# adaLN sums moved from VectorE to GpSimd, and 512-column products on [high | low] in the mixers and feed-forwards

## The chip, the cores and the metric

The kernel runs on one core of a Trainium2 chip. The metric is the device time of one execution in microseconds. The kernel before took 1213.28 us in the median of 3 runs (1211.68 to 1213.52).

## The reference, cut to what matters

Two layers, each a half-step SwiGLU feed-forward, a gated mixer of three attentions, and a second half-step feed-forward. Each of these six sub-layers is modulated by a vector `c` (adaLN), and the kernel numbers them as stages 0 to 5: 0, 2, 3 and 5 are feed-forwards, 1 and 4 mixers.

```python
D_MODEL = 1024; SEQ = 256; DEPTH = 2; D_FF = 2816        # batch 1, all float32

def swiglu(h, wg, wu, wd):
    return (jax.nn.silu(h @ wg) * (h @ wu)) @ wd
...
for l in range(DEPTH):
    mod = (jax.nn.silu(c) @ w_ada[l] + b_ada[l]).reshape(Bn, 3, 3, D_MODEL)[:, :, :, None, :]
    def pre(xx, j):
        return rmsnorm(xx, norm_gain[l, j]) * (1 + mod[:, j, 1]) + mod[:, j, 0]
    h = pre(x, 0)
    x = x + 0.5 * mod[:, 0, 2] * swiglu(h, w_ffn_gate[l, 0], w_ffn_up[l, 0], w_ffn_down[l, 0])
    h = pre(x, 1)
    (q_sb, k_sb, v_sb, q_dil, k_dil, v_dil, q_swa, k_swa, v_swa,
     g_sb, g_dil, g_swa) = jnp.split(h @ w_in[l], split_idx, axis=-1)
    ...
    merged = (jax.nn.sigmoid(g_sb) * (o_sb @ w_br_sb[l])
              + jax.nn.sigmoid(g_dil) * (o_dil @ w_br_dil[l])
              + jax.nn.sigmoid(g_swa) * (o_swa @ w_br_swa[l]))
    x = x + mod[:, 1, 2] * (merged @ w_out[l])
    h = pre(x, 2)
    x = x + 0.5 * mod[:, 2, 2] * swiglu(h, w_ffn_gate[l, 1], w_ffn_up[l, 1], w_ffn_down[l, 1])
return rmsnorm(x, final_gain)
```

## The kernel before, in words

Every large product is made of three: weights and activations are each split into a high half (rounded to fp32r) and a low half (the rest), and high x high, low x high and high x low are added in PSUM. Activations lie with features on the partitions and the 256 tokens as columns: `hH` and `hL`, 8 blocks of 128 features each.

The work comes in units. A column unit is 128 output features over all 1024 inputs, a row unit is 128 inputs over 1024 outputs. SyncE loads raw weights, two units at a time, into 3 buffers (`load_raws`, L133). `feed` makes the halves five units ahead (`AHEAD`): ScalarE casts `wH` (L150), VectorE subtracts `wL` (L158), 1024 columns each. `step` runs one unit: feed, one tick of the adaLN pace, the matmuls, then what was left over from the unit before, then this unit's own post-work.

A column unit (`aform`, L594) is 24 matmuls of 256 columns: for each of 8 blocks `wH` with `hH` and `wL` with `hH`, then 8 times `wH` with `hL`. In a feed-forward a gate and an up unit share a PSUM bank; the post-work after the up unit is a Silu from PSUM (L652), the product with the up half (L653), a cast to `ffH` (L656) and the low half `ffL` (L657). In a mixer two query, key or gate units share a bank. Row units (`run_rows`, L706) have 12 matmuls of 512 columns, with activations as the stationary side. The last four of them, `TAIL`, run output piece by output piece, so that the residual and the next norm can begin. In the norm, `rstd` (L464 to L467) uses GpSimd.

adaLN is 18 chunks of 1024 columns. The first two are made in a special opening; the other 16 come as 128 steps. A step (`ada_step`) loads 128 x 1024 of `w_ada` into one of two buffers (L260, SyncE), scales it by a column of silu(c) and adds it to an accumulator: ScalarE for the first of a chunk (L281), VectorE for the other seven (L283). A finished chunk is reduced over partitions on TensorE (`ada_reduce`): chunks listed in `filler` in a stage's tail, the others `SOON` ticks after the last step. `PACE` gives the weights by which a stage's steps are spread over its units; `N1` says how many tail reductions stand ahead of the second half's norm.

A `tile` name in the rows leaves buffer numbers out: `pf`, `pq`, `pg` are PSUM banks of feed-forward, query/key and gate units, `pd` those of row units, `acc` an adaLN accumulator, `ada` its load.

## Time and profile before

| | |
|---|---|
| median of 3 runs | 1213.28 us |
| the profiled execution | 1215.12 us |
| its span, first to last instruction | 1213.4 us |
| TensorE matmuls, weight loads busy | 1181.0 us (97%), 1102.9 us (91%) |
| VectorE, ScalarE, GpSimd busy | 837.3 us (69%), 616.0 us (51%), 19.0 us (2%) |
| DMA | 287.55 MB, 237 GB/s in the mean |

The page gives each engine's busy time, the granted clock and the DMA load over the span; the views of the trace give single groups, waits and stretches. The granted clock is a share of 2.4 GHz: 1.00 is that level, 0.50 the other, 1.2 GHz. Matmuls overlap, so that the mean duration of one is longer than the distance to the next; the distance is read from a long piece of the chain, time over count.

### The profile page before, as it was taken

How to read it: one execution, taken by the hardware profiler on the slowest of the kernel's cores; microseconds unless marked ns; L12 is line 12 of the kernel's file. 1: busy time of each engine (PE TensorE's matmuls, PEld its weight loads, DVE VectorE, ACT ScalarE, POOL GpSimd, SP SyncE). 2: the span in 40 equal slices, each digit the busy share in tenths (PEclk: the TensorE clock that was granted, in tenths of full speed). 3: DMA queues.
4: the chain of work that ended last, by engine and by line, in shares of the span. 5: the costliest groups of instructions: out<-in, count | busy, mean ns of one | idle time of the engine just before them, and what ended most of it. 6: DMA issues, size and time to landing. Idle time of an engine off the chain costs nothing.

```text
span 1213.4 us, 21101 instructions
## 1 busy us (share of the span) xinstructions
PE 1181.0 (97%) x8765; PEld 1102.9 (91%) x8765; DVE 837.3 (69%) x1087; ACT 616.0 (51%) x953; POOL 19.0 (2%) x38
## 2 busy tenths in 40 slices
PE   6999998899999999999999999999999999999997
PEld 5999986699999899999889999889999998999986
DVE  3677575878889888766577666567766788555544
ACT  5555343556555475444365444346655456444432
POOL 1000000000000000000000000000000000000000
PEclk9999999899999999999999999999999999999999
DMA  9999889698769959876738676748743584556550
GB/s 318 313 303 332 272 308 318 211 314 271 253 230 314 319 176 326 263 243 242 261 112 298 219 242 226 258 157 291 264 149 113 186 276 147 190 178 197 180 176 35
DMA packets 189671, 287.55 MB, mean 237 GB/s; under 512 B 6806, under 2 KB 155496, under 8 KB 189576
## 3 DMA queue, kind: packets, MB, share of 16 engines
q1 hardware_dynamic: 187656, 279.88, 68.8%
q0 software_dynamic: 1776, 6.14, 1.7%
q8 instruction: 68, 1.11, 0.4%
q14 instruction: 27, 0.22, 0.1%
q10 hardware_dynamic: 144, 0.20, 0.0%
HBM read 285.12 MB, written 3.42 MB: 238 GB/s over the span
## 4 chain that ended last, share of the span: by engine, by line
PE 85%; DMA 6%; DVE 3%; ACT 2%; issue 2%; POOL 1%; SPq 0%; POOLq 0%; ACTq 0%; DVEq 0%
PE pf L594 37%; PE pd L706 16%; PE pg L594 12%; PE pq L594 7%; DMA ada<-in_w_ada 5%; PE pb L594 3%; PE pf L624 3%; PE pv L942 2%; DVE acc L283 1%; DVE wL L158 1%; PE adaf L212 1%; DMA first<-in_w_ada 1%; PE psn L488 1%; ACT wH L150 1%; ACT jk L452 0%
## 5 line engine op out<-in xcount | busy, mean ns | idle before, releaser
L158 DVE TENSOR_TENSOR wL<-raw,wH 128x1024 fp32r<-128x1024 f32 (+1 forms) x384 | 461.8, 1211 | 224.8 <-ACT wH L150 224.3
L150 ACT CAST wH<-raw 128x1024 fp32r<-128x1024 f32 (+1 forms) x384 | 393.1, 1040 | 244.5 <-PE pd L706 90.1
L594 PE MATMUL pf<-hH,wH 128*128 128x256 f32 x1312 | 324.5, 285 | 0.4 <-DVE hH L505 0.4
L594 PE MATMUL pf<-hH,wL 128*128 128x256 f32 x1312 | 323.5, 284 | 0.0
L594 PEld LDWEIGHTS pf<-hH,wH 128*128 128x128 f32 x1312 | 253.1, 193 | 1.7 <-issue 0.9
L594 PEld LDWEIGHTS pf<-hH,wL 128*128 128x128 f32 x1312 | 253.5, 193 | 0.2 <-issue 0.2
L594 PE MATMUL pf<-hL,wH 128*128 128x256 f32 x1312 | 183.8, 283 | 0.0
L283 DVE SCALAR_TENSOR_TENSOR acc<-ada,sc,acc 128x1024 f32<-128x1024 f32 x112 | 143.4, 1280 | 40.6 <-DMA ada<-in_w_ada 40.6
L594 PEld LDWEIGHTS pf<-hL,wH 128*128 128x128 f32 x1312 | 169.1, 192 | 0.0
L706 PE MATMUL pd<-wL,ffH 128*128 128x512 f32 x336 | 132.7, 395 | 5.1 <-DVE wL L158 5.1
L706 PE MATMUL pd<-wH,ffH 128*128 128x512 f32 x336 | 132.5, 394 | 0.0
L706 PE MATMUL pd<-wH,ffL 128*128 128x512 f32 x336 | 132.2, 393 | 0.0
L594 PE MATMUL pg<-hH,wH 128*128 128x256 f32 x384 | 96.0, 288 | 0.0
L594 PE MATMUL pg<-hH,wL 128*128 128x256 f32 x384 | 94.0, 283 | 0.0
L652 ACT ACTIVATE sil<-pf 128x256 f32<-128x256 f32 x88 | 33.3, 382 | 98.4 <-PE pf L594 98.4
L706 PEld LDWEIGHTS pd<-wL,ffH 128*128 128x128 f32 x336 | 63.9, 190 | 19.3 <-DVE wL L158 6.2
L706 PEld LDWEIGHTS pd<-wH,ffH 128*128 128x128 f32 x336 | 63.9, 190 | 14.0 <-issue 0.8
L706 PEld LDWEIGHTS pd<-wH,ffL 128*128 128x128 f32 x336 | 64.0, 190 | 13.2
L594 PEld LDWEIGHTS pg<-hH,wH 128*128 128x128 f32 x384 | 73.5, 191 | 2.3 <-issue 0.9
L594 PEld LDWEIGHTS pg<-hH,wL 128*128 128x128 f32 x384 | 73.6, 192 | 0.0
L653 DVE TENSOR_TENSOR f<-pf,sil 128x256 f32<-128x256 f32 x88 | 36.9, 422 | 33.9 <-ACT sil L652 33.9
L594 PE MATMUL pq<-hH,wH 128*128 128x256 f32 x224 | 55.8, 287 | 0.0
(215 smaller groups left out, 1437.2 us busy)
## 6 DMA issues: line engine op xcount, KB each, us to landing
ada<-in_w_ada SPq DMA_DIRECT2D x128, 512.0 KB, 5.4
raw<-in_w_ffn_down SPq DMA_DIRECT2D x44, 1024.0 KB, 4.8
raw<-in_w_in SPq DMA_DIRECT2D x42, 1024.0 KB, 6.1
raw<-in_w_ffn_gate SPq DMA_DIRECT2D x41, 1024.0 KB, 6.1
raw<-in_w_ffn_up SPq DMA_DIRECT2D x41, 1024.0 KB, 5.8
first<-in_w_ada SPq DMA_DIRECT2D x32, 256.0 KB, 6.0
raw<-in_w_out SPq DMA_DIRECT2D x8, 1024.0 KB, 7.1
raw<-in_w_ffn_gate SPq DMA_DIRECT2D x12, 256.0 KB, 6.0
```

Source lines behind the costliest of these rows:

```text
L150: nc.scalar.copy(u.H, u.view(self.raw_tiles[u.raw]))
L158: nc.vector.tensor_tensor(u.L, u.view(self.raw_tiles[u.raw]), u.H, op=ALU.subtract)
L212: self.nc.tensor.matmul(self.first_ps[q % 2][32 * i:32 * i + 32, 0:P], w, src[:, i * P:(i + 1) * P], start=kb in (0, None), stop=kb == KB - 1)
L283: self.nc.vector.scalar_tensor_tensor(acc, src, sc, acc, ALU.mult, ALU.add)
L488: self.nc.tensor.transpose(p[:, i * P:(i + 1) * P], xn[:, fb * P:(fb + 1) * P], self.ident)
L594: nc.tensor.matmul(out, w[:, kb, cs], x[:, kb, :], start=i == 0, stop=i == n - 1)
L624: self.nc.tensor.matmul(ps[fb][:, S * up:S * up + S], w[:, 2 * k + up, b * P:(b + 1) * P], x[:, 2 * q + k, :], start=q == 0 and not up and ...
L652: nc.scalar.activation(sil, p[:, :S], AF.Silu)
L653: nc.vector.tensor_tensor(f32, p[:, S:], sil, op=ALU.mult)
L706: self.nc.tensor.matmul(out, x[:, kb, sl], w[:, 0, hs], start=first and i == 0, stop=last and i == 2)
L942: self.nc.tensor.matmul(out, x[:, 4 * (i % 2) + k, sl], w[:, k, :], start=i % 2 == 0 and j == 0, stop=i % 2 == 1 and j == n - 1)
```

## The change

Three things. The column units of all feed-forwards (except for the opening of the first) and of the mixers' queries, keys and gates use `wide`: `hH` and `hL` lie side by side in one tile `hHL`, and 8 matmuls of 512 columns take `wH` with both, into the two halves of a whole bank; 8 of 256 add `wL` with `hH` to the first half. `join` adds the halves afterwards, by a ScalarE copy and a VectorE add, one unit later. The first two units of stages 2, 3 and 5 keep 24 matmuls, in a high and a low part. The adaLN steps run on GpSimd, as a multiply and an add, with the next load issued one step later. And the tables that place the steps are new: `PACE`, `SPARE`, `SOON`, `N1`, and four chunks fewer in `filler`.

```diff
-N1 = (1, 3, 3, 2, 1, 0)
+N1 = (0, 1, 2, 2, 1, 0)
...
-PACE = ((1, 0.75, 1, 1.5), (0, 1.5, 1.5, 1, 0.75, 0.75), (2, 1.5, 1, 1), (1, 0.5, 1, 0.75), (1, 2, 0, 0, 1, 2),
-        (1, 1, 1, 1))
-SPARE = 1
-SOON = 5
+PACE = ((1, 1, 1, 0.75, 0), (0.5, 1, 1, 1, 1, 0), (1, 1, 1, 0.75, 0), (1, 1, 1, 0.75, 0), (0.5, 1, 1, 1, 1, 0),
+        (1, 1, 1, 1, 1))
+SPARE = (5, 1, 1, 1, 1, 1)
+SOON = 7
...
-        self.filler = {(1, 2): 0, (2, 2): 1, (3, 0): 1, (3, 1): 1, (3, 2): 2, (4, 0): 2, (4, 1): 2, (4, 2): 3,
-                       (5, 0): 3, (5, 2): 4}
+        self.filler = {(2, 2): 1, (3, 2): 2, (4, 0): 2, (4, 2): 3, (5, 0): 3, (5, 2): 4}
...
         if kb == 0:
-            self.nc.scalar.activation(acc, src, AF.Copy, scale=sc)
+            self.nc.gpsimd.tensor_scalar(acc, src, sc, None, ALU.mult)
         else:
-            self.nc.vector.scalar_tensor_tensor(acc, src, sc, acc, ALU.mult, ALU.add)
+            self.nc.gpsimd.tensor_scalar(src, src, sc, None, ALU.mult)
+            self.nc.gpsimd.tensor_tensor(acc, acc, src, op=ALU.add)
...
         self.ada_mac(i, t)
         self.ada_pos += 1
-        self.ada_load()
...
-        self.hH = self.sp.tile([P, KB, S], F32R, tag="hH", name=f"hH{s}", bufs=1)
-        self.hL = self.sp.tile([P, KB, S], F32R, tag="hL", name=f"hL{s}", bufs=1)
+        self.hHL = self.sp.tile([P, KB, 2, S], F32R, tag="hHL", name=f"hHL{s}", bufs=1)
+        self.hH, self.hL = self.hHL[:, :, 0, :], self.hHL[:, :, 1, :]
...
-        if self.pending:
-            self.pending()
-            self.pending = None
+        self.drain()
         if u.post:
-            self.pending = u.post()
+            self.pending.append(u.post)
...
+    def wide(self, u, bank, part="all"):
...
+        one, two = bank[:, :S], bank[:, S:]
+        kbs = range(u.shape[0])
+        both = self.hHL.rearrange("p k c n -> p k (c n)")
+        seq = {"all": [(bank, u.H, both, kb) for kb in kbs] + [(one, u.L, self.hH, kb) for kb in kbs],
+               "high": [(one, u.H, self.hH, kb) for kb in kbs] + [(one, u.L, self.hH, kb) for kb in kbs],
+               "low": [(two, u.H, self.hL, kb) for kb in kbs]}[part]
+        for i, (out, w, x, kb) in enumerate(seq):
+            self.nc.tensor.matmul(out, w[:, kb, :], x[:, kb, :], start=part != "low" and i == 0,
+                                  stop=part != "high" and i == len(seq) - 1, skip_group_check=True)
+
+    def join(self, out, bank):
+
+        self.nc.scalar.copy(out, bank[:, S:])
+        self.nc.vector.tensor_tensor(out, bank[:, :S], out, op=ALU.add)
...
+        def gate_post(fb):
+            def post():
+                sil = self.sil[:, fb % 3, :]
+                self.join(sil, ps[fb])
+                self.nc.scalar.activation(sil, sil, AF.Silu)
+            return post
...
+        def up_wide_post(fb):
+            def post():
+                f32 = self.f32[:, fb % 3, :]
+                self.join(f32, pu[fb])
+                self.nc.vector.tensor_tensor(f32, f32, self.sil[:, fb % 3, :], op=ALU.mult)
+                return split(fb, f32)
+            return post
...
             def post():
-                if f % 4 == 1:
+                if f % 4 == 0:
                     th[b, f // 4] = self.work([P, 4, S], f"th{s}_{b}_{f}")
-                i = f // 2
-                self.nc.scalar.activation(th[b, f // 4][:, 2 * (i % 2):2 * (i % 2) + 2, :],
-                                          gps[b, i].rearrange("p (b n) -> p b n", b=2), AF.Tanh, scale=0.5)
+                t = th[b, f // 4]
+                self.join(t[:, f % 4, :], gps[b, f])
+                if f % 2:
+                    two = t[:, f % 4 - 1:f % 4 + 1, :]
+                    self.nc.scalar.activation(two, two, AF.Tanh, scale=0.5)
...
-            need = 8 * (max(due) + 1) - self.ada_pos + SPARE
+            need = 8 * (max(due) + 1) - self.ada_pos + SPARE[s]
...
-                parts = [k // 4, k // 4, k - k // 4 * 2, NF - TAIL]
+                parts = [k // 4, k // 4, k - k // 4 * 2, NF - TAIL - 3, 3]
```

TensorE in the input loop of stage 2, the second feed-forward, before: the last rows of one gate unit and the first of the next (`pf_17`, `pf_18` are their banks).

```order
L594 MATMUL pf_17_5820<-hH_4604,wH_5713 128x256
L594 MATMUL pf_17_5820<-hH_4604,wL_5715 128x256
L594 MATMUL pf_17_5820<-hL_4605,wH_5713 128x256 x8
L594 MATMUL pf_18_5919<-hH_4604,wH_5748 128x256
L594 MATMUL pf_18_5919<-hH_4604,wL_5750 128x256
```

The same place now, two gate units and an up unit, whole (`pu` is an up unit's own bank).

```order
L611 MATMUL pf_16_5242<-hHL_4207,wH_5094 128x512 x8
L611 MATMUL pf_16_5242<-hHL_4207,wL_5096 128x256 x8
...
L611 MATMUL pf_17_5278<-hHL_4207,wH_5118 128x512 x8
L611 MATMUL pf_17_5278<-hHL_4207,wL_5120 128x256 x8
L611 MATMUL pu_16_5306<-hHL_4207,wH_5152 128x512 x8
L611 MATMUL pu_16_5306<-hHL_4207,wL_5154 128x256 x8
```

The alternation of `wH` and `wL` over 16 rows, and the 8 behind it, became 8 of double width and 8 of `wL`.

VectorE in the same loop before, about one pair of blocks (`f` is the product of gate and up).

```order
L653 TENSOR_TENSOR f_4730<-pf_10_5396,sil_4729 128x256
L158 TENSOR_TENSOR wL_5489<-raw_5327,wH_5487 128x1024
L657 TENSOR_TENSOR ffL_4728<-f_4730,ffH_4727 128x256
L653 TENSOR_TENSOR f_4730<-pf_11_5430,sil_4729 128x256
L158 TENSOR_TENSOR wL_5521<-raw_5327,wH_5519 128x1024
L283 SCALAR_TENSOR_TENSOR acc_0_5226<-ada_5360,sc,acc_0_5226 128x1024
L657 TENSOR_TENSOR ffL_4728<-f_4730,ffH_4727 128x256
L158 TENSOR_TENSOR wL_5557<-raw_5394,wH_5555 128x1024
```

VectorE there now.

```order
L617 TENSOR_TENSOR sil_4312<-pf_11_4927,sil_4312 128x256
L158 TENSOR_TENSOR wL_4980<-raw_4831,wH_4978 128x1024
L617 TENSOR_TENSOR f_4313<-pu_10_4958,f_4313 128x256
L683 TENSOR_TENSOR f_4313<-f_4313,sil_4312 128x256
L158 TENSOR_TENSOR wL_5008<-raw_4831,wH_5006 128x1024
L690 TENSOR_TENSOR ffL_4311<-f_4313,ffH_4310 128x256
L617 TENSOR_TENSOR f_4313<-pu_11_4986,f_4313 128x256
L683 TENSOR_TENSOR f_4313<-f_4313,sil_4312 128x256
```

The sums (L283) are gone from between the `wL`; the joins (L617) came in, and the product of gate and up (L683) now has both inputs in SBUF.

GpSimd before, from the end of the first mixer to the end of stage 2: it has nothing but the norms' `rstd`.

```order
L466 TENSOR_TENSOR r_0_4563<-ms_0_4539 128x1
L467 TENSOR_TENSOR r_0_4563<-r_0_4563,mhalf 128x1
L467 TENSOR_TENSOR r_1_4661<-r_1_4661,mhalf 128x1
L466 TENSOR_TENSOR r_0_6545<-ms_0_6521 128x1
L467 TENSOR_TENSOR r_0_6545<-r_0_6545,mhalf 128x1
```

GpSimd now, at the end of the first mixer and the beginning of stage 2.

```order
L283 TENSOR_TENSOR acc_2_3640<-acc_2_3640,ada_3935 128x1024
L465 TENSOR_TENSOR r_0_4166<-ms_0_4142 128x1
L466 TENSOR_TENSOR r_0_4166<-r_0_4166,mhalf 128x1
L466 TENSOR_TENSOR r_1_4251<-r_1_4251,mhalf 128x1
L280 TENSOR_SCALAR acc_0_4333<-ada_3991,sc 128x1024
L282 TENSOR_SCALAR ada_4331<-ada_4331,sc 128x1024
L283 TENSOR_TENSOR acc_0_4333<-acc_0_4333,ada_4331 128x1024
```

The `rstd` of a norm stands behind all the steps of its stage; between the norms of stages 0 to 5 there are 29, 27, 32, 24, 16 and no steps.

## Rows read from the trace of the kernel before

**Rows 1.** The page: busy us and share of the span, by engine.

```profile
PE 1181.0 (97%) x8765; PEld 1102.9 (91%) x8765; DVE 837.3 (69%) x1087; ACT 616.0 (51%) x953; POOL 19.0 (2%) x38
```

**Rows 2.** TensorE's waits: us in total, times, longest.

```profile
PE pd L706 <- DVE wL L158: 5.1, 2, 4.4
```

**Rows 3.** The chain that ended last: start us, us, what, count.

```profile
119.18 1.72 PE adag L344 x4
...
433.27 126.94 PE pf L594 x1056
560.20 54.44 PE pd L706 x240
```

**Rows 4.** TensorE's groups of L594 by loop: busy us, mean ns, idle before.

```profile
L594 PE MATMUL pf<-hH,wH 128*128 128x256 f32 x1312 | 324.5, 285 | 0.4 <-DVE hH L505 0.4
...
L594 PE MATMUL pg<-hH,wH 128*128 128x256 f32 x384 | 96.0, 288 | 0.0
...
L594 PE MATMUL pq<-hH,wH 128*128 128x256 f32 x224 | 55.8, 287 | 0.0
```

**Rows 5.** PE, PEld, DVE, ACT, POOL busy us by stretch; granted clock, DMA share, GB/s.

```profile
212.00:221.00 9.00, 6.75 (x15) 4.88 (x16) 6.26 (x6) 1.90 (x2) 0.00 (x0) 0.50 0.91 290
300.00:400.00 100.00, 100.00 (x832) 95.94 (x832) 89.19 (x123) 56.30 (x102) 0.00 (x0) 1.00 0.80 273
433.00:560.00 127.00, 127.00 (x1059) 126.94 (x1058) 94.18 (x118) 68.25 (x101) 0.00 (x0) 1.00 0.79 266
...
1016.00:1145.00 129.00, 128.57 (x1059) 128.42 (x1058) 77.86 (x102) 65.10 (x98) 0.00 (x0) 0.99 0.58 188
```

**Rows 6.** In order of time, end of stage 0: start us, us, [idle before].

```profile
208.77 0.39 PE L706 MATMUL pd<-wH,ffH 128*128 128x512 f32 x1
...
211.09 1.28 DVE L283 SCALAR_TENSOR_TENSOR acc<-ada,sc,acc 128x1024 f32<-128x1024 f32 x1 [2.87 <-DMA ada<-in_w_ada]
...
213.57 0.80 PE L706 MATMUL pd<-wL,ffH 128*128 128x512 f32 x1 [4.41 <-DVE wL L158]
```

**Rows 7.** VectorE's groups: busy us, mean ns, idle before and its releaser.

```profile
L158 DVE TENSOR_TENSOR wL<-raw,wH 128x1024 fp32r<-128x1024 f32 x372 | 451.6, 1222 | 218.2 <-ACT wH L150 217.7 <-DMA first<-in_w_ada 0.2
L283 DVE SCALAR_TENSOR_TENSOR acc<-ada,sc,acc 128x1024 f32<-128x1024 f32 x112 | 143.4, 1280 | 40.6 <-DMA ada<-in_w_ada 40.6
L653 DVE TENSOR_TENSOR f<-pf,sil 128x256 f32<-128x256 f32 x88 | 36.9, 422 | 33.9 <-ACT sil L652 33.9
```

**Rows 8.** ScalarE's group of that shape from PSUM, the same columns.

```profile
L652 ACT ACTIVATE sil<-pf 128x256 f32<-128x256 f32 x88 | 33.3, 382 | 98.4 <-PE pf L594 98.4
```

**Rows 9.** GpSimd in order of time, in the first and the last norm.

```profile
226.00 0.54 POOL L466 TENSOR_TENSOR r<-ms 128x1 f32<-128x1 f32 x1 [108.55 <-ACT jk L452]
...
1201.96 0.18 POOL L466 TENSOR_TENSOR rf<-ms 128x1 f32<-128x1 f32 x1 [186.85 <-ACT jk L452]
1202.22 0.56 POOL L467 TENSOR_TENSOR rf<-rf,mhalf 128x1 f32<-128x1 f32 x1
```

**Rows 10.** VectorE at the same two places.

```profile
225.80 0.69 DVE L536 TENSOR_TENSOR x<-x,y 128x512 f32<-128x512 f32 x1
...
1201.72 0.68 DVE L535 SCALAR_TENSOR_TENSOR y<-pd,gate 128x512 f32<-128x512 f32 x1
1202.43 0.69 DVE L536 TENSOR_TENSOR x<-x,y 128x512 f32<-128x512 f32 x1
```

**Rows 11.** GpSimd's groups with the most columns, and one of one column.

```profile
L385 POOL TENSOR_SCALAR_AFFINE_SELECT sbm<-sbm 128x128 f32<-128x128 f32 x1 | 0.3, 282 | 0.0
masks.py:197 POOL MEMSET ident<- 128x128 f32 x1 | 0.2, 205 | 0.3 <-POOLq L1338 0.3
...
L1338 POOL MEMSET const-float32-0.0<- 128x1 f32 x1 | 0.1, 98 | 0.3 <-issue 0.3
```

**Rows 12.** The adaLN loads (L260): us to landing, and SyncE's wait for buffers.

```profile
DMA to landing us min/median/max: 3.2/5.4/19.4
...
SPq L260 <- DVE acc L283: 129.4, 76, 3.5
```

More of the change, by code (lines that the diff above doesn't have):

```diff
@@ L573, in step, with drain @@
         self.done()
-        if self.pending:
-            self.pending()
-            self.pending = None
+        self.drain()
         if u.post:
-            self.pending = u.post()
+            self.pending.append(u.post)
+    def drain(self):
+        todo, self.pending = self.pending, []
+        for f in todo:
+            later = f()
+            if callable(later):
+                self.pending.append(later)
     def flush(self):
-        if self.pending:
-            self.pending()
-            self.pending = None
+        while self.pending:
+            self.drain()
     def aform(self, u, out, xh, xl, off=0, part="all"):
@@ L609, in plan_ffn @@
         plan = {"kind": "ffn", "s": s, "in": [], "out": []}
-        ps = {}
+        ps, pu = {}, {}
         def start_pe(b0, q):
@@ L639, in pe, with split, later @@
                     ps[fb] = self.ps(f"pf{s}_{fb}")
-                self.aform(u, ps[fb][:, :S], self.hH, self.hL, part=part)
+                self.wide(u, ps[fb], part)
             return pe
-        def up_pe(fb):
-            return lambda u: self.aform(u, ps[fb][:, S:], self.hH, self.hL)
+        def gate_post(fb):
[4 more added lines that the diff above has]
+            return post
+        def up_pe(fb):
+            def pe(u):
+                pu[fb] = self.ps(f"pu{s}_{fb}")
+                self.wide(u, pu[fb])
+            return pe
+        def up_wide_post(fb):
[5 more added lines that the diff above has]
+            return post
+        def split(fb, f32):
+            def later():
+                self.nc.scalar.copy(self.ffH[:, fb, :], f32)
+                self.nc.vector.tensor_tensor(self.ffL[:, fb, :], f32, self.ffH[:, fb, :], op=ALU.subtract)
+            return later
         def up_post(fb):
@@ L653, in post @@
                 nc.vector.tensor_tensor(f32, p[:, S:], sil, op=ALU.mult)
-                def later():
-                    nc.scalar.copy(self.ffH[:, fb, :], f32)
-                    nc.vector.tensor_tensor(self.ffL[:, fb, :], f32, self.ffH[:, fb, :], op=ALU.subtract)
-                return later
+                return split(fb, f32)
             return post
@@ L678, in plan_ffn @@
             rg, ru = self.col_raw(wg, ((q * 256, 256),)), self.col_raw(wu, ((q * 256, 256),))
-            for r, mk in ((rg, gate_pe), (ru, up_pe)):
+            for r, mk, post in ((rg, gate_pe, gate_post), (ru, up_pe, up_wide_post)):
                 for b in range(2):
@@ L682, in plan_ffn @@
                     view = lambda t, b=b: t.rearrange("p (k n) -> p k n", k=KB)[:, :, b * P:(b + 1) * P]
-                    u = Unit(r, view, (KB, P), mk(fb), up_post(fb) if r == ru else None)
+                    u = Unit(r, view, (KB, P), mk(fb), post(fb))
                     self.units.append(u)
@@ L726, in run_rows @@
             self.done()
-            self.flush()
+            self.drain()
+        self.flush()
         for c in LATE:
@@ L807, in run_ffn @@
             self.done(2)
+            self.pending += [u.post for u in us]
         for i, u in enumerate(plan["in"]):
@@ L814, in run_ffn @@
                 self.bias_table()
-        self.flush()
         self.run_rows(plan["out"], s, self.ffH, self.ffL, early)
@@ L834, in pe, with qk_post @@
             def pe(u):
-                if i % 2 == 0:
-                    ps[i // 2] = self.ps(f"pq{s}_{i}")
-                self.aform(u, ps[i // 2][:, (i % 2) * S:(i % 2 + 1) * S], self.hH, self.hL)
+                ps[i] = self.ps(f"pq{s}_{i}")
+                self.wide(u, ps[i])
             return pe
-        def qk_post(q):
+        def qk_post(i):
             def post():
                 nc = self.nc
-                p = ps[q]
-                dst = self.qk[:, 2 * q:2 * q + 2, :]
-                src = p.rearrange("p (b n) -> p b n", b=2)
-                nc.scalar.copy(dst, src)
-                if q == 6:
-                    nc.scalar.copy(self.qk[0:64, 14, :], p[64:128, S:])
-                    nc.scalar.copy(self.qk[64:128, 14, :], p[0:64, S:])
+                self.join(self.qk[:, i, :], ps[i])
+                if i == 13:
+                    nc.scalar.copy(self.qk[0:64, 14, :], self.qk[64:128, 13, :])
+                    nc.scalar.copy(self.qk[64:128, 14, :], self.qk[0:64, 13, :])
             return post
@@ L854, in plan_mixer @@
             for b in range(2):
-                u = Unit(r, half(b), (KB, P), qk_pe(2 * q + b), qk_post(q) if b else None)
+                u = Unit(r, half(b), (KB, P), qk_pe(2 * q + b), qk_post(2 * q + b))
                 self.units.append(u)
@@ L863, in pe @@
             def pe(u):
-                if f % 2 == 0:
-                    gps[b, f // 2] = self.ps(f"pg{s}_{b}_{f}")
-                self.aform(u, gps[b, f // 2][:, (f % 2) * S:(f % 2 + 1) * S], self.hH, self.hL)
+                gps[b, f] = self.ps(f"pg{s}_{b}_{f}")
+                self.wide(u, gps[b, f])
             return pe
@@ L917, in plan_mixer @@
                     f = f0 + i
-                    u = Unit(r, half(i), (KB, P), g_pe(b, f), g_post(b, f) if i else None)
+                    u = Unit(r, half(i), (KB, P), g_pe(b, f), g_post(b, f))
                     self.units.append(u)
@@ L1194, in run_mixer @@
                 fn(arg)
-        self.flush()
         self.run_rows(plan["out"], s, self.mH, self.mL)
@@ L1199, in run @@
         nc, a = self.nc, self.a
-        self.pending = None
+        self.pending = []
         self.ada_setup()
```

## The prediction

> **What bounds the kernel now.** I read the busy times first. TensorE's matmul row is busy 97% of the span [rows 1], and past the opening it waited for little: the largest entry is 5.1 us, two waits for VectorE's low halves `wL` [rows 2]. So the kernel is a stream of matmuls and the question is what one of them costs. The chain of waits gives that in its long pieces [rows 3]: in a feed-forward's input loop 1056 matmuls of 256 columns take 126.94 us, 120.2 ns each; in its output loop 240 matmuls of 512 columns take 54.44 us, 226.8 ns each. Two of 256 columns cost 240.4 ns, one of 512 costs 226.8, so each matmul carries about 13.6 ns that doesn't scale with columns. This is the handle of the change. Then the other engines by stretch [rows 5]: VectorE is busy 89% of the first mixer's gate part, 74% of the second feed-forward's input loop, 60% of the last one's, which has no adaLN sums. VectorE has room in places, not everywhere. Last, the one real stall, at the end of the first feed-forward: a matmul starts at 208.77 us and the next one at 213.57; its `wL` came late because VectorE stood 2.87 us in front of an adaLN sum whose load hadn't landed, with the `wL` queued behind it [rows 6]. Behind it the clock was granted at 1.2 GHz: the stretch 212 to 221 reads 0.50 [rows 5].
>
> **The wide products.** There are (1312 + 384 + 224) / 8 = 240 column units in the three loops [rows 4], each of 24 matmuls: 24 x 120.2 ns = 2.885 us. A wide unit is 8 of 512 and 8 of 256: 8 x 226.8 + 8 x 120.2 = 2.776 us, so it saves 0.109 us. Six units (the first two of the three later feed-forwards) run in a high and a low part and keep 24 matmuls. 234 x 0.109 = 25.6 us, all on the path, as TensorE is the path.
>
> **A rule on that.** The row's fixed part is 13.6 ns a matmul. The Trainium skill, page TensorE: Matmul & The Clock Gate, section Back-to-back issue gap, puts the lone gap at columns / 2.4 plus about 2.5 ns. By it the change would save 8 x 2.5 x 234, an estimate of 4.7 us; the rows here stand against it.
>
> **The joins.** Each of the 240 units now ends in a ScalarE copy of 256 columns and a VectorE add of PSUM and SBUF. Nearest rows: 382 ns for the Silu of that shape from PSUM, 422 ns for the product with one PSUM input [rows 7, 8]. That is 240 x 0.42 = 101 us on VectorE and 92 us on ScalarE, where some copies of the mixers' projections go in return; VectorE loses 143.4 us of adaLN sums [rows 7]. Per block of a feed-forward (a gate and an up unit, 5.55 us of TensorE) VectorE has 2 x 1.22 + 2 x 0.42 for joins + 0.42 + 0.42 = 4.12 us, 74%: as full as the second feed-forward is today, which ran without a stall [rows 5]. In the first mixer's gate part a unit gives up about one sum, 1.28 us, and takes 0.42. The cover is VectorE's idle 26% and the five units that the halves are made ahead. The posts come a block later, so ScalarE no longer stands at a Silu for the unit just issued. The price left on the path is banks: each unit takes a PSUM bank of its own where two shared one, and in the mixers, which also use three banks for each attention step, TensorE may wait for a join. No row shows this. Below it is nothing; above, one join's add of 0.42 us behind each of the 24 attention steps that take banks (12 a mixer), 10 us. I take 4 us.
>
> **The sums on GpSimd.** 112 sums become a multiply and an add of 1024 columns each, 16 a multiply alone. No row shows such an operation. From below, a memset goes from 98 ns at one column to 205 at 128, 0.84 ns a column, about 0.95 us for 1024 [rows 11]: 1.9 us a step. From above, a select of 128 columns takes 282 ns, eight of them 2.3 us: 4.5 us a step. I take the middle, 3.2 us. 128 steps are then about 380 us of an engine that is idle 98% of the time, so its busy time costs nothing by itself. What counts is the pace. By the tables the first feed-forward runs 29 steps over 32 units and three quarters of that weight on 15 rows: 0.67 a unit, a step every 4.1 us. The second runs 32 over 44 + 11.25 units, a step every 4.8 us; the third 24, every 6.4 us; the first mixer 27, about every 5 us. A step of 3.2 us fits all of them. Behind a late step stand on GpSimd the norm's `rstd` operations and the bias table's DMAs, on SyncE the next sum's load, which waits for the buffer, and every weight load after it, and on TensorE the reductions seven units later. The last rows of each stage have no steps, so `rstd` should find GpSimd free.
>
> **The shared SBUF port.** GpSimd is held up by VectorE: the sum of two one-column vectors takes 0.54 us where it starts during `x<-x,y`, whose inputs both lie in SBUF, and 0.18 us during `y<-pd,gate`, which has one in PSUM [rows 9, 10]. The first ended at 226.54, right behind the VectorE operation's end at 226.49. The other direction: at 1202.43 `x<-x,y` started while GpSimd was 0.2 us into a 0.56 us operation and took its usual 0.69 us [rows 9, 10]. So GpSimd waits and VectorE, on this one small case, doesn't. I take that: a step grows by up to two waits of 1.22 us behind `wL`, half of each on average, to 4.4 us, about the pace of the first feed-forward and below the others'. I allow 4 us for what SyncE then holds back in the first feed-forward.
>
> **Places.** Sums no longer sit in VectorE's queue before `wL`, and there are 29 instead of 33 in the first feed-forward, 2 MB less. The stall at its end (4.4 + 0.7 us, and 4.5 us lost to half clock over 9) should shrink; I take half, 5 us, since GpSimd can hold the same loads up in another way; ends nothing and 10. Four chunks' reductions leave the tails, where they filled TensorE's wait for the norm, and run amid the units: two matmuls of a gate chunk are 0.86 us [rows 3], so at most 3.4 us, taken as 3.
>
> **Sum.** -25.6 + 4 + 4 - 5 + 3 = -19.6 us. The profiled execution took 1215.12 us around its span of 1213.4, the median is 1.8 below it: 1215.1 - 19.6 - 1.8 = 1193.7, so 1194. With the ends: -25.6 - 10 + 3 = -32.6 gives 1181; -25.6 + 10 + 4 + 3.4 = -8.2 gives 1205.
>
> **Rival 1: the port holds VectorE too.** If a GpSimd operation that reads SBUF also holds back each VectorE operation with two SBUF inputs, the two share the time. Per feed-forward block VectorE has 2 x 1.22 + 0.42 + 0.42 = 3.28 us of those. With 1.34 steps of 3.2 us in the first (4.3 us) a block needs 7.6 us against 5.55, 16 blocks lose 33 us; in the second 1.16 steps, 7.0 us, 22 blocks lose 32; in the third 0.87, 6.06 us, 11. That is 76 us; the five units made ahead can absorb 5 x 2.776 = 14 us in each of the three, 42 in all. So 34 to 76 us in the place of the 4 taken above: 1224 to 1266, slower. It decides from a step of (5.55 - 3.28) / 1.16 = 2.0 us in the second feed-forward on. For it: the lock is visible in one direction and my price is above 2.0. Against it: the 0.69 us beside GpSimd, and that the step's lower end is 1.9 us. The Trainium skill, page SBUF — State Buffer, section Who interferes with whom, states just this: a VectorE operation with two SBUF inputs and a GpSimd operation that reads SBUF exclude each other for a whole instruction, whoever comes first. Half of it the rows show, the other half they contradict on one tiny operation. Chance 0.33.
>
> **Rival 2: the load chain is too slow.** There are two buffers for the sums' loads, and a load now goes out only with the next step. A buffer turns over in the load's landing, 5.4 us at the median and up to 19.4 [rows 12], plus the step: (5.4 + 4.4) / 2 = 4.9 us a step against 4.1 in the first feed-forward, 29 x 0.8 = 23 us, or with landings of 8 us, as the DMAs are busiest there, 29 x 2.1 = 61 us, less 14 absorbed each. SyncE already stood 129.4 us for such buffers without TensorE suffering [rows 12], which speaks against it. 9 to 47 us for the 4: 1199 to 1237, mostly near 1208. Chance 0.12, of which 0.05 ends faster, 0.05 same, 0.02 slower.
>
> **Rival 3: it doesn't do what it says.** If in the column loops 120.2 ns is already all columns, so that a matmul of 512 takes 240 there, the 25.6 us go: 1220, slower. If a fifth of the fixed part were real, about 5 of them would be left: 1215, no change. Against both stands the output loop's own pitch [rows 3]. By the page's 2.5 ns above it would be this second case. Chance 0.05: 0.03 slower, 0.02 same.
>
> **How the numbers follow.** The forecast has 0.50. What a measurement of this kernel can tell from no change is about 0.2%, 2.4 us. Faster: 0.50 + 0.05 = 0.55; same: 0.05 + 0.02 = 0.07; slower: 0.33 + 0.02 + 0.03 = 0.38. The range goes from the forecast's lower end, 1181, to 1250, which leaves out the upper part of rival 1 (about 0.12) and little below; the forecast's own range is 1181 to 1205.
>
> **What would show it.** Right: wide matmuls at 227 ns and units of 2.78 us in the chain; `wL` still at 1.22 us beside GpSimd; TensorE's waits under 30 us in sum; no stall near 210 us. Wrong: `wL` of 2 us and more with TensorE waiting for it (rival 1); SyncE standing for `acc` or `ada` on GpSimd, and ScalarE's casts waiting for weight loads in the first 230 us (rival 2); wide matmuls at 240 ns (rival 3). A multiply and an add together above 4.5 us would break the price of a step.

## The result, and the profile after

The changed kernel takes 1305.34 us in the median of 4 runs (1303.93 to 1310.0), the kernel before 1212.96 beside it. The ratio is 1.077, with a 95% interval from 1.0741 to 1.0799: **7.7% slower**. The forecast was 1194 us, the range ended at 1250. The profiled execution took 1310.0 us, its span 1308.0.

Busy us and share of the span by engine, after (before: [rows 1]), and under it the shares of the chain that ended last, by engine.

```profile
PE 1200.5 (92%) x6893; PEld 1027.8 (79%) x6893; DVE 969.9 (74%) x1215; ACT 657.9 (50%) x1163; POOL 752.2 (58%) x278
...
PE 52%; POOL 14%; DVE 14%; issue 9%; ACT 6%; DMA 5%; SPq 0%; POOLq 0%; ACTq 0%; DVEq 0%
```

TensorE has 19.5 us more of busy time than before, although it does fewer and wider matmuls, and 107.5 us of the span without work against 32.4 before. The chain runs over TensorE for 52% of the span only (85% before); GpSimd and VectorE have 14% each. The page of before shows those shares as follows.

```profile
PE 85%; DMA 6%; DVE 3%; ACT 2%; issue 2%; POOL 1%; SPq 0%; POOLq 0%; ACTq 0%; DVEq 0%
```

Now by stage: each of these windows goes from the first norm transpose of a stage (`psn`) to that of the next, the first from the start, the last to the end. Columns: busy us of PE, PEld, DVE, ACT, POOL, granted clock, DMA share, GB/s.

```profile
0.00:256.80 256.80, 210.01 (x1333) 179.25 (x1333) 163.97 (x192) 110.52 (x187) 171.10 (x73) 0.93 0.80 262
256.80:475.80 219.00, 205.83 (x1233) 177.30 (x1233) 178.66 (x222) 114.96 (x212) 160.38 (x55) 0.95 0.64 217
475.80:697.50 221.70, 199.45 (x1038) 169.10 (x1036) 178.99 (x192) 105.37 (x185) 187.34 (x63) 0.95 0.69 234
697.50:906.20 208.70, 198.14 (x1037) 167.59 (x1037) 162.45 (x192) 104.65 (x184) 138.88 (x48) 0.96 0.66 231
906.20:1108.00 201.80, 196.80 (x1235) 170.30 (x1233) 156.89 (x224) 115.10 (x212) 91.66 (x34) 0.99 0.59 201
1108.00:1308.00 200.00, 190.28 (x1027) 164.22 (x1025) 128.97 (x197) 107.25 (x188) 2.86 (x5) 0.98 0.48 161
```

The table compares the stages' lengths in the profiled executions, read at the same transposes, with the runs that come below.

| us | stage 0 | 1 | 2 | 3 | 4 | 5 |
|---|---|---|---|---|---|---|
| steps on GpSimd, after | 29 | 27 | 32 | 24 | 16 | 0 |
| sums by the tables of before (before, e9, e10, e17) | 33 | 39 | 24 | 16 | 16 | 0 |
| before | 228.0 | 198.0 | 193.0 | 193.0 | 197.6 | 203.8 |
| after | 256.8 | 219.0 | 221.7 | 208.7 | 201.8 | 200.0 |
| no adds (e6) | 227.9 | 196.4 | 193.9 | 191.6 | 196.2 | 199.5 |
| a second multiply for the add (e7) | 258.3 | 203.1 | 212.8 | 191.9 | 196.2 | 198.8 |
| adds alone (e8) | 238.7 | 211.9 | 211.7 | 204.9 | 202.6 | 200.1 |
| wide alone, all else as before (e17) | 246.1 | 214.1 | 195.5 | 189.7 | 196.3 | 200.9 |

The loss goes with the steps: 29, 21, 29, 16 and 4 us where there are steps, and a gain of 4 where there are none. The clock adds to it: the mean granted clock is 0.959 against 0.992, which, if the rest runs at full level, is 107 us at the half level (2 x 0.041 x 1308) against 19.

What a step costs. GpSimd's groups: busy us, mean ns, idle before.

```profile
L282 POOL TENSOR_SCALAR ada<-ada,sc 128x1024 f32<-128x1024 f32 x112 | 399.4, 3566 | 197.2 <-DMA ada<-in_w_ada 197.1
L283 POOL TENSOR_TENSOR acc<-acc,ada 128x1024 f32<-128x1024 f32 x112 | 283.2, 2529 | 9.3
```

The same two lines by themselves: ns at the least, in the middle and at the most.

```profile
L282 POOL TENSOR_SCALAR ada<-ada,sc x112: 2837/3816/4883, 78.2 to 1082.4; 128x1024 f32<-128x1024 f32 x112
...
L283 POOL TENSOR_TENSOR acc<-acc,ada x112: 2337/2412/3473, 82.2 to 1085.3; 128x1024 f32<-128x1024 f32 x112
```

A step takes 2.84 + 2.34 = 5.2 us undisturbed and 3.57 + 2.53 = 6.1 in the mean; the prediction had 3.2, and 4.4 with its waits. Stage 0's 29 steps (four of them a multiply alone) begin at 75.3 us and end at 255.0; GpSimd is busy with them for 164.5 of these 180 us, and stage 0 ended at 256.8. The chain says the same: its shares by line from 78 to 256.

```profile
by line: POOL ada L282 43.4%; POOL acc L283 31.6%; DMA ada<-in_w_ada 15.2%; issue 7.2%; POOL acc L280 4.1%; DMA row<-mk 2.0%; POOL scr L432 0.6%; POOL r L466 0.3%; POOL r L465 0.2%; POOLq L280 0.0%; POOLq L282 0.0%; POOLq L465 0.0%
```

No TensorE work stands in it; three quarters are multiplies and adds. Its end, on GpSimd, then ScalarE, then TensorE (start us, us, idle before and its releaser):

```profile
249.25 3.30 POOL L282 TENSOR_SCALAR ada<-ada,sc 128x1024 f32<-128x1024 f32 x1
252.64 2.34 POOL L283 TENSOR_TENSOR acc<-acc,ada 128x1024 f32<-128x1024 f32 x1
254.94 0.38 POOL L465 TENSOR_TENSOR r<-ms 128x1 f32<-128x1 f32 x1
255.39 0.57 POOL L466 TENSOR_TENSOR r<-r,mhalf 128x1 f32<-128x1 f32 x1
...
255.99 0.72 ACT L474 ACTIVATE xn<-x,r 128x512 f32<-128x512 f32 x1 [5.34 <-POOL r L466]
...
256.77 0.47 PE L487 MATMUL psn<-ident,xn 128*128 128x128 f32 x1 [4.11 <-ACT xn L474]
```

ScalarE had read its sum of squares at 250.66 (250.47 + 0.19), but the norm's `rstd` stood behind two operations of a step, and TensorE behind it, 4.11 us. TensorE's waits over the span:

```profile
PE adam L352 <- POOL acc L283: 29.8, 4, 19.9
PE adam L358 <- ACT acc L354: 19.9, 5, 5.6
PE adag L343 <- POOL acc L283: 7.7, 1, 7.7
...
PE pd L749 <- DVE wL L158: 2.8, 5, 0.8
```

The longest, 19.9 us, ends at 178.97: a reduction that TensorE meets in its order, while the chunk's last add runs until 178.91. Three such waits lie in stage 0 (7.7, 19.9 and 3.4 us), 31.0 of the 35 us that TensorE stood there after 70 us. SyncE's two largest waits; the first was 129.4 us in the kernel before [rows 12], the second, for `wL`, 582.8:

```profile
SPq L259 <- POOL acc L283: 291.8, 68, 9.7
SPq L133 <- DVE wL L158: 254.1, 58, 21.8
```

And the port. VectorE's low halves by themselves ([rows 7] had 1222 ns in the mean), ns at the least, in the middle and at the most:

```profile
L158 DVE TENSOR_TENSOR wL<-raw,wH x384: 692/1224/3426, 18.5 to 1284.8; 128x1024 fp32r<-128x1024 f32 x186, 128x768 fp32r<-128x768 f32 x4, 128x512 fp32r<-128x512 f32 x2
```

The product of gate and up, now with both inputs in SBUF (busy us, mean ns; 424 ns at the least):

```profile
L683 DVE TENSOR_TENSOR f<-f,sil 128x256 f32<-128x256 f32 x82 | 82.3, 1004 | 2.8
```

GpSimd and VectorE at two places in order of time (start us, us):

```profile
203.72 2.44 POOL L283 TENSOR_TENSOR acc<-acc,ada 128x1024 f32<-128x1024 f32 x1
203.82 3.42 DVE L158 TENSOR_TENSOR wL<-raw,wH 128x1024 fp32r<-128x1024 f32 x1
206.15 3.81 POOL L282 TENSOR_SCALAR ada<-ada,sc 128x1024 f32<-128x1024 f32 x1
...
328.10 2.41 POOL L283 TENSOR_TENSOR acc<-acc,ada 128x1024 f32<-128x1024 f32 x1
328.88 2.72 DVE L158 TENSOR_TENSOR wL<-raw,wH 128x1024 fp32r<-128x1024 f32 x1
331.52 0.41 DVE L617 TENSOR_TENSOR qkv<-pq,qkv 128x256 f32<-128x256 f32 x1
```

The `wL` at 203.82 begins 0.1 us into an add. It ends at 207.24; less its own 1.22 us it got going at 206.02, 0.14 before the add's end. The multiply that began at 206.15, in the remaining `wL`, takes 3.81 for 2.84: it waits in its turn. The second place shows the same (331.60 - 1.22 = 330.38, the add's end is 330.51). The join beside it, with one input in PSUM, keeps its 0.41. Over all VectorE operations that began during a GpSimd operation and were lengthened (157), those in an add get going 0.14 us before its end in the median, those in a multiply 1.88 us before its end. So an add holds the port for 2.2 of its 2.34 us and a multiply for about 0.96 of its 2.84.

### The profile page after: what moved, and what is told of

It reads as the page before. It is cut to its first block, busy times and chain, and to the rows that moved or that the text cites. A ratio compares the mean times of both kernels' runs of the same rounds, so it can differ in the third digit from the quotient of the medians.

```text
span 1308.0 us, 18070 instructions
## 1 busy us (share of the span) xinstructions
PE 1200.5 (92%) x6893; PEld 1027.8 (79%) x6893; DVE 969.9 (74%) x1215; ACT 657.9 (50%) x1163; POOL 752.2 (58%) x278
## 3 DMA queue, kind: packets, MB, share of 16 engines
HBM read 285.12 MB, written 3.42 MB: 221 GB/s over the span
## 4 chain that ended last, share of the span: by engine, by line
PE 52%; POOL 14%; DVE 14%; issue 9%; ACT 6%; DMA 5%; SPq 0%; POOLq 0%; ACTq 0%; DVEq 0%
PE pf L611 11%; PE pu L611 10%; PE pd L749 10%; POOL ada L282 7%; DVE wL L158 7%; PE pq L611 6%; PE pg L611 5%; POOL acc L283 5%; DMA ada<-in_w_ada 3%; ACT wH L150 3%; PE pv L983 2%; PE pf L647 2%; PE pb L598 1%; DVE ffL L690 1%; POOL acc L280 1%
## 5 line engine op out<-in xcount | busy, mean ns | idle before, releaser
L282 POOL TENSOR_SCALAR ada<-ada,sc 128x1024 f32<-128x1024 f32 x112 | 399.4, 3566 | 197.2 <-DMA ada<-in_w_ada 197.1
L283 POOL TENSOR_TENSOR acc<-acc,ada 128x1024 f32<-128x1024 f32 x112 | 283.2, 2529 | 9.3
L611 PE MATMUL pf<-hHL,wH 128*128 128x512 f32 (+1 forms) x704 | 172.2, 388 | 1.0 <-DVE hHL L504 1.0
L611 PE MATMUL pu<-hHL,wH 128*128 128x512 f32 x656 | 172.0, 406 | 0.7 <-ACT wH L150 0.7
L611 PEld LDWEIGHTS pf<-hHL,wH 128*128 128x128 f32 x704 | 125.2, 194 | 24.8 <-DVE hHL L504 1.7
L611 PEld LDWEIGHTS pu<-hHL,wH 128*128 128x128 f32 x656 | 122.5, 196 | 25.2 <-issue 1.3
L611 PE MATMUL pg<-hHL,wH 128*128 128x512 f32 x384 | 99.2, 400 | 0.7 <-DVE modv L365 0.4
L611 PEld LDWEIGHTS pf<-hHL,wL 128*128 128x128 f32 x656 | 91.0, 194 | 6.6 <-DVE wL L158 0.5
L611 PE MATMUL pf<-hHL,wL 128*128 128x256 f32 x656 | 93.0, 285 | 0.0
L611 PE MATMUL pu<-hHL,wL 128*128 128x256 f32 x656 | 92.3, 284 | 0.0
L683 DVE TENSOR_TENSOR f<-f,sil 128x256 f32<-128x256 f32 x82 | 82.3, 1004 | 2.8
```

The costliest lines, as they stand in the source:

```text
L282: self.nc.gpsimd.tensor_scalar(src, src, sc, None, ALU.mult)
L283: self.nc.gpsimd.tensor_tensor(acc, acc, src, op=ALU.add)
L611: self.nc.tensor.matmul(out, w[:, kb, :], x[:, kb, :], start=part != "low" and i == 0, stop=part != "high" and i == len(seq) - 1, skip_gro ...
L683: self.nc.vector.tensor_tensor(f32, f32, self.sil[:, fb % 3, :], op=ALU.mult)
```

## The experiments

**Which part.** First the two large parts apart. e1 takes the sums back to ScalarE and VectorE and leaves the rest of the change; e2 leaves out the wide products.

```diff
-            self.nc.gpsimd.tensor_scalar(acc, src, sc, None, ALU.mult)
+            self.nc.scalar.activation(acc, src, AF.Copy, scale=sc)
...
-            self.nc.gpsimd.tensor_scalar(src, src, sc, None, ALU.mult)
-            self.nc.gpsimd.tensor_tensor(acc, acc, src, op=ALU.add)
+            self.nc.vector.scalar_tensor_tensor(acc, src, sc, acc, ALU.mult, ALU.add)
```

> The changed kernel with its tables and wide products, but each adaLN sum as one VectorE operation (the first of a chunk on ScalarE), as before the change. Theory A (late sums: a GpSimd step takes 5.2 us alone and 6.1 in the profile, where the stages ask for one every 4.1 to 6.4) and theory B (the port: VectorE operations with two SBUF inputs are held up, some 170 us in sum) both expect the loss gone: 1190 to 1220 us, VectorE near full in the feed-forwards (4.12 + 1.16 x 1.28 = 5.6 us a block against 5.59 of TensorE). Theory C (the wide products: joins, banks of their own) expects it to stay: over 1270.

Measured: 1296.42 us, ratio 1.0693 (1.0671 to 1.0714). Theories A and B miss; the time is where theory C, the wide products, had it.

e2 is the kernel before with the sums on GpSimd, the later load, and all tables of the change.

```diff
+            self.nc.gpsimd.tensor_scalar(src, src, sc, None, ALU.mult)
+            self.nc.gpsimd.tensor_tensor(acc, acc, src, op=ALU.add)
...
-        self.ada_load()
```

> The kernel before with the adaLN steps on GpSimd and the changed tables, and no wide products. A and B expect the loss in full and the wide gain missing: 1305 to 1330 us. C expects 1215 to 1230.

Measured: 1297.36 us, 1.0691 (1.0659 to 1.0723). That is below the range of A and B and far above that of C. The sums on GpSimd, with the later load and the new tables, cost 85 us with no wide product in the kernel, so the joins aren't needed for the loss. But e1 loses as much without the sums on GpSimd. Two things fail, each by itself, and together they cost hardly more than one.

e11 is the kernel before with the new tables alone (`N1`, `PACE`, `SPARE`, `SOON`, `filler`).

> The kernel before with the changed tables alone (pace, spare, soon, norm order, filler): sums on VectorE, column units of 24 matmuls. If the tables are a minor matter: 1212 to 1230. If they alone explain the wide kernel with VectorE sums (1296): over 1270, and then the wide products cost nothing.

Measured: 1215.48 us, 1.0031 (1.0018 to 1.0044): 0.3%, not the cause by themselves.

**Which property of a step: its length or its hold on the port.** Three edits of the step's two lines. e6 leaves the adds out; e7 puts a second multiply in the place of the add, so that a step stays as long and holds the port less; e8 leaves the multiplies out, so that a step is short and holds the port nearly all the time. The three make other sums than the reference.

e6:

```diff
-            self.nc.gpsimd.tensor_tensor(acc, acc, src, op=ALU.add)
```

> The changed kernel without the adds of the adaLN sums: GpSimd scales each load in place and the accumulator keeps the first block alone. A step is 2.9 to 3.6 us of GpSimd, which every stage's pace allows, and holds the port 0.96 us. A expects 1190 to 1220 us, near the run with the adds alone. B expects 0.96 / 3.2 of the loss: 1215 to 1240, and some 40 us less than the run with the adds alone.

e7:

```diff
-            self.nc.gpsimd.tensor_tensor(acc, acc, src, op=ALU.add)
+            self.nc.gpsimd.tensor_scalar(src, src, sc, None, ALU.mult)
```

> The changed kernel with the add of each adaLN step replaced by a second multiply in place, so the sums keep one block alone. A multiply takes 2.84 us and in the changed kernel's trace lets waiting VectorE operations go after 0.96 of it; an add takes 2.34 and holds them for 2.2. So a step is as long as in the changed kernel (5.7 us and more) but holds the port 1.9 us instead of 3.2. Theory A (the step is too long for the pace, sums and loads come late) expects 1285 to 1315 us, with TensorE waiting for GpSimd. Theory B (the held port) expects 1206 + 0.96 / 2.2 x 99 = 1250 at most, 1220 where short holds find cover.

e8:

```diff
-            self.nc.gpsimd.tensor_scalar(src, src, sc, None, ALU.mult)
```

> The changed kernel without the multiplies of the adaLN sums: GpSimd adds the loads unscaled, all but the first. A step is 2.4 to 3.5 us, which every pace allows, and holds the port 2.2 us. A expects 1200 to 1215, as the run without adds (1206). B expects 1206 + (2.2 - 0.96) / 2.2 x 99, about 1260.

Measured: e6 1206.12 us (0.9939, 0.9917 to 0.9962), e7 1265.96 (1.045, 1.0424 to 1.0476), e8 1267.3 (1.0451, 1.0412 to 1.0491). Taking the adds out gives back 99 us and makes the change a small gain. e6 is where theory A had it and e8 a little above where theory B had it, while e7 lies between the two; e7 and e8 lie about 60 us above e6. So neither theory was the whole. The shares of the chain by engine tell them apart. e7:

```profile
PE 52%; POOL 29%; DMA 8%; DVE 4%; issue 3%; ACT 3%; SPq 0%; POOLq 0%; ACTq 0%; DVEq 0%
```

e8:

```profile
PE 59%; DVE 19%; issue 9%; ACT 6%; DMA 5%; POOL 2%; POOLq 0%; SPq 0%; ACTq 0%; DVEq 0%
```

In e7 GpSimd is on the chain for 29% of the span: late steps. Its loss is mostly in stages 0 and 2, where the most steps are asked for. In e8 GpSimd is busy 30% and on the chain for 2%; it is VectorE there, lengthened by the port: the loss is spread over stages 0 to 3, and even the 16 steps of stage 4 cost 6 us. Stage 3 tells them apart best: its 24 steps ask for one every 6.4 us, which a step of 6.1 meets. There e7 loses nothing against e6 (191.9 and 191.6 us), and e8 loses 13 (204.9). The changed kernel has both, 14% and 14%; if the two losses, 60 and 61, can be added at all, they overlap, as the adds' whole price is 99.

e4 moves the multiply to ScalarE, in place, and leaves the add on GpSimd.

```diff
-            self.nc.gpsimd.tensor_scalar(src, src, sc, None, ALU.mult)
+            self.nc.scalar.activation(src, src, AF.Copy, scale=sc)
```

> The changed kernel with each adaLN multiply on ScalarE and only the add on GpSimd. A step on GpSimd is then 2.4 to 3.5 us, which every stage's pace allows, but it still holds the port 2.2 us of the 3.2 it held. A expects most of the loss gone: 1195 to 1225 us, no wait of TensorE for GpSimd's sums. B expects 2.2 / 3.2 of the loss to stay: 1260 to 1280.

Measured: 1361.88 us, 1.1246 (1.1209 to 1.1283), the slowest of all. It doesn't settle what it was meant to, since it adds a wait: ScalarE now stands for the sums' loads and buffers in front of its casts. TensorE's waits for ScalarE's `wH` are 25.3 us at `pu` and 12.3 at `pf`, under 1 us each in the changed kernel, and its waits for ScalarE at the reductions are 50.7 us for 19.9.

**The places.** e15 puts the reductions of four chunks back into the tails (`filler`, `N1` of before), e18 issues the next load right after a step again.

e15:

```diff
-        self.filler = {(2, 2): 1, (3, 2): 2, (4, 0): 2, (4, 2): 3, (5, 0): 3, (5, 2): 4}
+        self.filler = {(1, 2): 0, (2, 2): 1, (3, 0): 1, (3, 1): 1, (3, 2): 2, (4, 0): 2, (4, 1): 2, (4, 2): 3,
+                       (5, 0): 3, (5, 2): 4}
```

> The changed kernel with one thing put back: the reductions of the four chunks that had left the stages' tails stand in the tails again (filler and N1 of before); the sums stay on GpSimd with the changed pace. Theory A (late sums cost mainly because TensorE, in order, stands at a reduction amid the units until GpSimd and then ScalarE have finished): the waits for acc, 57 us in the changed kernel, and a part of the half clock behind them go, 1225 to 1250. Theory B (a reduction is only where the lateness shows; weight halves and loads are late by as much, and TensorE stands at the next unit instead): 1285 to 1310.

e18:

```diff
         self.ada_mac(i, t)
         self.ada_pos += 1
+        self.ada_load()
```

> The changed kernel with the next load issued right after a step again, as before the change; all else as changed. Theory A (the later load is a part of the loss: GpSimd stood 197 us for loads, and a step that starts late makes all behind it late): GpSimd's wait for loads falls, 1260 to 1290. Theory B (the load stood later for a reason: SyncE now waits for the GpSimd step in progress with the weight loads queued behind it, and the length of a step, 5.2 to 6.1 us, stays what it is): 1300 to 1330, with SyncE standing longer than 292 us for acc on GpSimd.

Measured: e15 1337.54 us (1.1036, 1.1018 to 1.1055), e18 1313.27 (1.0832, 1.0812 to 1.0853). e15 is worse than either theory had it: stages 2 and 3 get shorter (206.6 and 192.7 us), but 0 and 1 grow to 294.8 and 238.6. TensorE still waits for `acc` on GpSimd, 34.8 us at `adam` and 14.2 at `adag`, and 12.5 for the norm's `xn`. But `filler` also says by when a chunk is due, so e15 moved steps as well: its stages 0 to 4 run 37, 35, 24, 17 and 15 of them, where the changed kernel runs 29, 27, 32, 24 and 16. The stages with eight more steps grew by 38 and 20 us, those with eight and seven fewer shrank by 15 and 16. So e15 speaks for the number of steps in a stage and doesn't tell what the reductions' place costs. e11 bears on that: with the sums on VectorE, the new places cost at most the 3.3 us of all its tables. e18 goes by theory B: SyncE stands 324.5 us for `acc` on GpSimd (291.8 before that edit), GpSimd's multiplies wait less for loads (172.4 for 197.1 us), and the time is not better, which fits a limit in the length of a step.

**Why the wide products lose with the sums on VectorE.** e17 is the kernel before with the wide products and joins and nothing else; e19 is e1 with the next load right after a step, so only the tables are new.

> The kernel before with the wide products and joins in all loops of the change, and nothing else: sums on ScalarE and VectorE as before, tables and load order of before. Theory A (joins and 1.28 us sums together leave VectorE, and ScalarE that waits for it, no room, so the earlier run of wide products with sums on VectorE was slow for that): 1270 to 1300. Theory B (that run was slow by the changed tables and the load that goes out a step later): 1190 to 1205.

> Wide products and sums on ScalarE and VectorE, with the changed tables, but the next load issued right after a step. It stands between two earlier runs: 1296 with the changed tables and the late load, 1238 with tables and load order of before. Theory A (the late load made that difference, as VectorE stands at a sum whose load hasn't landed with the weights' low halves behind it): 1235 to 1250, VectorE's wait for the loads from 64 back to about 28 us. Theory B (the tables made it, since they put more steps and reductions amid the column units where joins and sums already crowd): 1280 to 1300.

Measured: e17 1238.39 us (1.0213, 1.0197 to 1.0228), e19 1246.06 (1.0281, 1.026 to 1.0302). For e17 neither theory was right; there are two losses. Of e1's 84 us some 50 are the later load, as theory A for e19 said: VectorE stood at sums whose load hadn't landed, with the low halves queued behind them. VectorE's group of sums in e1:

```profile
L282 DVE SCALAR_TENSOR_TENSOR acc<-ada,sc,acc 128x1024 f32<-128x1024 f32 x112 | 143.4, 1281 | 63.8 <-DMA ada<-in_w_ada 63.6
```

And in e19:

```profile
L282 DVE SCALAR_TENSOR_TENSOR acc<-ada,sc,acc 128x1024 f32<-128x1024 f32 x112 | 143.3, 1280 | 8.2 <-DMA ada<-in_w_ada 8.2
```

Of the other 34, 8 are what e19 has over e17, the tables, and 26 are joins and sums beside each other. They go with the number of sums: +18 and +16 us in stages 0 and 1, which have 33 and 39 of them, +2.5 in stage 2 with 24, and gains of 1 to 3 us in stages 3, 4 and 5 with 16, 16 and none. What happens there is read from e17's chain in stage 0 (start us, us, what).

```profile
113.39 1.28 DVE acc L283
114.67 0.34 DVE ffL L691
115.01 0.35 DVE sil L618
...
115.70 1.04 ACT wH L150
...
116.76 0.34 DVE wL L158
...
117.91 0.43 DVE sil L618
...
118.68 1.04 ACT wH L150
...
120.89 1.28 DVE acc L283
```

A join's add waits in VectorE's order behind a sum; ScalarE waits in its order at the Silu for that add, and its next cast behind the Silu; VectorE's next low half waits for the cast. The chain goes to and fro between the two engines and TensorE isn't in it. Yet each engine is free a part of the time. Busy us of PE, PEld, DVE, ACT, POOL in e17 from 75 to 200 us:

```profile
75.00:200.00 125.00, 108.28 (x541) 88.58 (x541) 91.43 (x126) 61.17 (x108) 1.68 (x2) 0.95 0.78 258
```

VectorE is busy 73%, ScalarE 49%, and TensorE is without work for 17 of the 125 us. In the kernel before, in the same window, VectorE was busy 71% and TensorE without work for 0.8 us: the busy share hardly differs. Of the 17 us, 7.9 are two waits at reductions for a late sum (5.4 and 2.5) and most of the rest waits for weight halves. The sums' loads are on e17's chain too, after 138 us above all; how much of the 26 us is the exchange between the engines and how much late loads wasn't measured apart.

**Where it does pay.** e9 is the kernel before with wide products and joins in stage 5 alone, which has no sums, e10 in stages 3 and 5. `WIDE` is a new list of stages; all else is the code of the change for a feed-forward.

```diff
+WIDE = (3, 5)
...
-                    u = Unit(r, view, (KB, P), mk(fb), up_post(fb) if r == ru else None)
+                    u = Unit(r, view, (KB, P), (mkw if wide else mk)(fb),
+                             post(fb) if wide else up_post(fb) if r == ru else None)
```

> The kernel before with wide products and joins in the last feed-forward alone, where no adaLN sums run: 42 wide units, each 0.09 us shorter as the changed kernel's chain shows. If joins find cover there: 1213 - 3.8 = 1209 us. If the exchange of joins between ScalarE and VectorE slows the units even without sums: 1213 to 1225.

> The kernel before with wide products and joins in stages 3 and 5 alone. Stage 5 has no sums, and alone it gave 3.9 us; stage 3 has 24 sums over its 44 column units. If the joins fit beside a sum every 6.4 us, another 42 units x 0.09 us, 1204 to 1206; if joins and sums on VectorE don't go together even at that pace, above 1212.

Measured: e9 1208.36 us (0.9972, 0.9963 to 0.9981; before 1212.23 beside it), e10 1204.99 (0.9942, 0.9929 to 0.9954; before 1211.87). Both times came as expected; e10 is faster than both kernels, by 0.6% against the kernel before. But its expectation had a condition wrong: by the tables of before stage 3 has 16 sums, not 24, one about every 10 us in the column loops and not every 6.4. So the joins are shown to fit beside sums at that pace alone. e10's chain in stage 5:

```profile
1112.97 5.59 PE pf L617 x32
1118.55 5.59 PE pu L617 x32
```

Each piece is two units, 2.795 us a unit, against 2.885 before. 42 units x 0.09 = 3.8 us; e9 gained 3.9.

## Why the prediction was wrong, point by point

Two steps failed above all: the price of a step on GpSimd with the pace that followed from it, and "GpSimd waits and VectorE, on this one small case, doesn't", by which the sum had only 4 us, for what SyncE then holds back. In the place of those 4 us the sums on GpSimd cost 85 us without wide products (e2), and in the changed kernel their adds alone cost 99 (e6). The cover for the joins failed too, where many sums run on VectorE.

**The wide products: right, a little small.** 2.776 us a unit was forecast, 2.795 measured, so 0.09 instead of 0.109; 234 units would be 21 us for the 25.6 of the sum (234 x 0.109 is 25.5). A wide matmul then takes (2795 - 8 x 120.2) / 8 = 229 ns, against 240.4 for two narrow ones: 11 ns saved. The Trainium skill's fixed part that the prediction weighed (TensorE: Matmul & The Clock Gate, Back-to-back issue gap, about 2.5 ns) is given there for a lone matmul; this stream shows more than four times as much, so here the measurement decides. Rival 3 is out.

**The joins: the duration right, the path wrong.** The adds took 0.41 us as forecast. The step that failed is "The cover is VectorE's idle 26% and the five units that the halves are made ahead." The idle share was no cover for work that is passed between two engines which each work in order. With the sums of before beside them the joins cost about 26 + 21 = 47 us (e17, with what late loads add to it, and if the wide products saved their 21 there), for the 4 in the sum. That the sums had left VectorE was no rescue either, by the next points. The banks, for which the 4 us stood, show little: in e17 TensorE waits 4.8 us for the joins of gate units.

**The price of a step: the term that was mis-sized most.** 3.2 us were taken, 5.2 are needed, 6.1 were used. It lies outside the bounds, 1.9 to 4.5: the multiply alone, 2.84 us, is above the 2.3 that eight selects stood for. A select of another kind and width was no upper end for it. The Trainium skill, page GPSIMD Engine Reference, section Elementwise — side-by-side cycle accounting, has 4497 ns for an add of 2048 columns; half of it, an estimate of 2.25 us, would have met the add (2.34), and the prediction did not use it; no multiply like this one is priced in that section. "A multiply and an add together above 4.5 us would break the price of a step" was the prediction's own sign, and it came.

**The pace: failed with the price.** "A step of 3.2 us fits all of them" was compared with a step every 4.1, 4.8, 6.4 and about 5 us. At 6.1 only the third feed-forward's pace is met (and e7 loses nothing there). What stood behind a late step was named rightly: `rstd`, SyncE's weight loads, the reductions. "The last rows of each stage have no steps, so `rstd` should find GpSimd free" fails with it: a backlog fills the empty rows, and the rows above show `rstd` 4 us late. e7, a step as long with less of the port, ends at 1266.

**The port: "GpSimd waits and VectorE, on this one small case, doesn't" is false for large operations.** It came from one GpSimd operation of one column, which says nothing on one of 1024. The lock goes both ways, for nearly a whole add and a third of a multiply. The Trainium skill, SBUF — State Buffer, section Who interferes with whom, has the lock as exclusive for a VectorE operation with two SBUF inputs and a GpSimd operation that reads SBUF, and says of VectorE's 2-port modes that whoever issues first has it for the whole instruction. Here, where the VectorE operations have two inputs, the trace shows nearly a whole instruction for the add (2.2 of 2.34 us), and a shorter hold for the multiply (0.96 of 2.84). By luck the port time of a step, 3.16 us, is what the prediction took for the whole step, so rival 1's 34 to 76 us are close to what the adds by themselves cost: 61 (e8).

**The stall near 210 us and the fillers.** In the row units TensorE's waits for `wL` are 2.8 us in all, 0.8 at the longest, where that stall was 4.4, so it is gone as forecast. In its place stage 0 has 31.0 us of waits for late sums and 4.1 for the norm, and it ends 29 us later. The 3 us for the reductions that left the tails fit e11, where all tables together cost 3.3 with the sums in time. With the sums late, TensorE stands at reductions amid the units, 57.4 us over the span (29.8, 19.9 and 7.7 in the rows above).

**The rivals and the range.** Rival 1 (chance 0.33) named the port rightly. Rival 2 (0.12) was right that sums and loads come late, but reckoned with the loads' landings and a step of 4.4 us; loads that go out at once gained nothing (e18), and the longer step was what counted. Each had too small a time. Above all they were handled as alternatives that exclude each other, while a longer step feeds both. Both at once had no case, and the range ended at 1250, inside rival 1's own 1266.

**Still open.** Not all of e6's 1206.12 is accounted for: the wide products' 21 us are there in part, about 7 net. The new tables took 3.3 in e11; how the rest is divided between joins, multiplies on the port and loads wasn't measured. Nor was the reductions' place with the sums on GpSimd, as e15 moved steps too.

## What to carry to other kernels

An operation that is moved to an engine which the trace doesn't show doing it needs a measured price first, and that price is held against the pace that each stage asks for; a backlog reaches everything queued on that engine and on the queue that loads for it. Two engines that work in order and hand each other pieces can hold up a loop while both are busy less than three quarters of the time, as e17's chain shows for a stretch. Put a cheap gain where there is slack in order, not slack in the mean: here two stages of six gave 0.6%, all of them with the moved sums lost 7.7%.
